# An encoder block on one core: SSD decay moved off GpSimd, skip factors in the vector load, the last units by token tile, VectorE's order at the FFN's entry

## The chip, the core and the metric

The kernel runs on one core of a Trainium2 chip. Its engines each work through a queue of their own, in order: TensorE (PE in the profile) for matrix products, with its weight loads shown as PEld; VectorE (DVE), ScalarE (ACT) and GpSimd (POOL) for elementwise work; SyncE (SP), which here only issues DMAs. The metric is the device time of one execution in microseconds (us).

## What is computed

One layer of a hybrid encoder on 256 tokens of width 2048, in float32. Cut to what matters here:

```python
h = rms_norm(x, norm_mix_pre)
q, k, v, z, xbc, dt, g_sb, g_ssd = split(h @ w_in)
o_sb = stick_breaking_attention(q, k, v)               # 16 heads x 128
xs, bm, cm = split(silu(causal_dwconv(xbc, ...)))      # 64 heads x 64, 8 groups
dt = softplus(dt + dt_bias); a = -exp(a_log)
# SSD: decay = exp(cs_i - cs_j) where j <= i, else 0 (cs: cumulative sum of dt * a)
y = ssd_scan(xs, dt, a, bm, cm)                        # (cm.bm * decay) @ (xs * dt) per head
y = rms_norm_per_group((y + xs * d_skip) * silu(z))
merged = sigmoid(g_sb) * (o_sb @ w_sb_proj) + sigmoid(g_ssd) * (y @ w_ssd_proj)
x = x + rms_norm(merged @ w_out, norm_mix_post)
h = rms_norm(x, norm_ffn_pre)
gate, val = split(causal_dwconv(h @ w_up, ...))        # 2 x 5632
x = x + rms_norm((gelu(gate) * val) @ w_down, norm_ffn_post)
```

## The kernel before

**Weights.** All weights stream once, as 715 units of 128x1024 floats. A unit is loaded by SP (`raw`), rounded by ACT to `whi` (L63) and completed by VectorE with the rest, `wlo` = raw - whi (L64); both halves go to PE, which makes a float32 product of three faster ones. `unit()` (L97) hands a unit to PE's code and has three more prepared ahead; five buffers hold raw units, five hold split ones.

**Products.** `tok_mm` (L136) gives tokens by features: two PSUM banks, one for each token tile t of 128 tokens, three products for each step of 128 inputs and each t (L145 to L147), 12 for a unit. `feat_mm` (L115) gives features by tokens with pairs of products (L112, L113), 8 pairs for a unit; each pair needs both token tiles of its activations. `feat_mms` (L123) runs over the four chunks of its activations in the outer loop, two banks inside.

**Order.** PE's queue is as the program writes it. On the other engines a scheduler of the framework orders the work, save inside `manual_schedule`, where ACT and VectorE keep the written order: at the start (L189), at the FFN's entry (L619) and at the end (L713). Work on the side is written as generators; `pump()` (L155) advances the first of them by one `yield` after each four steps of `tok_mm`, or after a `feat_mm`.

**Stages.** Start: x is loaded in four chunks and multiplied by the norm's gain (`a`); x by tokens (`xt`) comes later for the statistics; ten products on `wake` keep PE busy meanwhile. Then eight SSD groups: `feat_mm` for xs and for B and C (`bc`), `tok_mm` for z, and beside ps_z the generator `ssd_work` (L323). In it PE transposes xs into px; `xw` = px * dt; `xd` (shown as xs) = px * d_skip, a copy on ACT and a product on GpSimd; `mm` is made from csb - cs by a subtraction (L338), masked by GpSimd's affine_select (L339), run through Exp on ACT as one 128x2048 operation (L347) and multiplied by pcb = B.C on VectorE (L350). ACT copies a part of pcb into `xw` (L345), the operand of po (L353). po carries the state of the first token tile to the second, pd (L363) is the part inside a tile. csb is the cumulative sum, spread over partitions by a DMA through DRAM. Then gates, attention, merging, and ps_mo, the product with w_out.

**The FFN's entry** (L618 to L652). After the last ps_mo: squares of its two banks (`n1.add`, n_j), `last` (n_v, then Ln and Exp on ACT), `newton` (three small operations on VectorE) give `n1.r`. Then for each feature block n and token tile t: mog = mog * r + xg (L632), transposed by PE (pth), rounded by ACT and completed by VectorE into the activations `h` (L64). ps_f, the first two tiles of the FFN, follow. x itself (xn, L647) and its statistics come after.

**The tail** (L713 to L727). After the last ps_fo: squares of both banks, `gained` (L701), `last`, `newton`, nine adds (L726), each with a store of its block, from ACT's queue and SP's in turn.

## Time and profile before

| | us |
|---|---|
| median of three runs | 2100.75 (2100.36 to 2102.08) |
| the profiled run's own time | 2101.31 |
| its span | 2099.6 |
| PE busy | 2072.1 (99%) |
| VectorE busy | 1386.0 (66%) |
| ACT busy | 1156.9 (55%) |
| GpSimd busy | 152.3 (7%) |

The span runs from the first instruction to the last; the profiled run's time has 1.7 us around it. Busy PE is not PE at its peak: where the clock is granted at half, products take twice as long and count as busy. In the rows below L12 is line 12 of the kernel, x4 a count of instructions merged into one row, and the brackets tell how long the engine stood before the row and what ended that.

### The profile page before, as it was taken

To read this page: it belongs to the slowest core of one execution; us is meant where nothing else is said; L and a number is where in the kernel's file an instruction comes from. 1 tells how busy PE (TensorE), PEld (TensorE's weight loads), DVE (VectorE), ACT (ScalarE), POOL (GpSimd) and SP (SyncE) were. 2 spreads that over 40 slices of the span, in tenths; PEclk is the share of its full clock that TensorE was granted. 3 is DMA by queue.
4 is the path that set the end of the run, shared out by engine and by line. 5 is a ranking of instruction groups with operands and counts; after the bars stand their busy time and mean duration, and the time that the engine had idled before them with its cause. 6 is when DMAs were issued, how large, how long until landed. Compare 5 with 4: busy or idle time off the path is not lost.

```text
span 2099.6 us, 27950 instructions
## 1 busy us (share of the span) xinstructions
PE 2072.1 (99%) x10632; PEld 1760.7 (84%) x10632; DVE 1386.0 (66%) x1794; ACT 1156.9 (55%) x1542; POOL 152.3 (7%) x134
## 2 busy tenths in 40 slices
PE   9999999999999999999999999999999999999997
PEld 7788888888888888888888888788888888888886
DVE  6888877788544445555544566598878887854443
ACT  6767677667543334555556444475555555544442
POOL 0222102222000000000000021100000000000000
PEclk9999999999999999999999999999999999999999
DMA  8564565555555555555555746475555555565653
GB/s 297 194 205 160 190 205 186 176 199 179 187 197 192 192 194 186 180 171 171 170 172 185 274 161 210 141 250 191 189 190 190 189 189 190 191 232 202 195 193 109
DMA packets 109094, 402.79 MB, mean 192 GB/s; under 512 B 12416, under 2 KB 12672, under 8 KB 106656
## 3 DMA queue, kind: packets, MB, share of 16 engines
q1 hardware_dynamic: 104912, 380.07, 54.1%
q0 software_dynamic: 3328, 20.02, 2.7%
q8 instruction: 83, 1.36, 0.3%
q10 hardware_dynamic: 720, 0.93, 0.1%
q14 instruction: 51, 0.42, 0.1%
HBM read 396.71 MB, written 4.26 MB: 191 GB/s over the span
## 4 chain that ended last, share of the span: by engine, by line
PE 92%; POOL 2%; DVE 2%; issue 2%; DMA 1%; ACT 1%; SPq 0%; DVEq 0%; ACTq 0%; POOLq 0%
PE ps_fv L112 8%; PE ps_fg L112 8%; PE ps_qk L112 6%; PE ps_xs L112 5%; PE ps_fo L147 4%; PE ps_fo L145 4%; PE ps_fo L146 4%; PE ps_fg L113 4%; PE ps_fv L113 4%; PE ps_qk L113 3%; PE ps_ssd L147 3%; PE ps_ssd L145 3%; PE ps_ssd L146 3%; PE ps_xs L113 2%; PE ps_bc L112 2%; PE ps_z L146 2%
## 5 line engine op out<-in xcount | busy, mean ns | idle before, releaser
L64 DVE TENSOR_TENSOR wlo<-raw,whi 128x1024 fp32r<-128x1024 f32 (+1 forms) x715 | 905.1, 1270 | 601.2 <-ACT whi L63 600.6
L63 ACT CAST whi<-raw 128x1024 fp32r<-128x1024 f32 (+1 forms) x715 | 746.2, 1051 | 793.7 <-PE ps_fo L147 128.9
L112 PE MATMUL ps_fg<-h,whi 128*128 128x512 f32 x688 | 240.7, 394 | 0.0
L112 PE MATMUL ps_fv<-h,whi 128*128 128x512 f32 x688 | 240.6, 394 | 0.0
L113 PE MATMUL ps_fg<-h,wlo 128*128 128x256 f32 x688 | 190.6, 277 | 0.0
L113 PE MATMUL ps_fv<-h,wlo 128*128 128x256 f32 x688 | 190.6, 277 | 0.0
L112 PE MATMUL ps_qk<-a,whi 128*128 128x512 f32 x512 | 181.3, 398 | 0.0
L112 PE MATMUL ps_xs<-a,whi 128*128 128x512 f32 x464 | 162.9, 396 | 0.0
L112 PEld LDWEIGHTS ps_fv<-h,whi 128*128 128x128 f32 x688 | 129.0, 188 | 30.0
L112 PEld LDWEIGHTS ps_fg<-h,whi 128*128 128x128 f32 x688 | 129.0, 188 | 30.0
L113 PE MATMUL ps_qk<-a,wlo 128*128 128x256 f32 x512 | 143.5, 280 | 0.0
L145 PE MATMUL ps_fo<-whi,f 128*128 128x512 f32 x352 | 136.9, 389 | 0.0
L147 PE MATMUL ps_fo<-whi,f 128*128 128x512 f32 x352 | 136.9, 389 | 0.0
L146 PE MATMUL ps_fo<-wlo,f 128*128 128x512 f32 x352 | 136.9, 389 | 0.0
L113 PEld LDWEIGHTS ps_fg<-h,wlo 128*128 128x128 f32 x688 | 129.2, 188 | 0.0
L113 PEld LDWEIGHTS ps_fv<-h,wlo 128*128 128x128 f32 x688 | 129.2, 188 | 0.0
L113 PE MATMUL ps_xs<-a,wlo 128*128 128x256 f32 x464 | 129.0, 278 | 0.0
L112 PEld LDWEIGHTS ps_qk<-a,whi 128*128 128x128 f32 x512 | 96.1, 188 | 22.6
L145 PE MATMUL ps_z<-whi,a 128*128 128x512 f32 x256 | 103.7, 407 | 0.0
L112 PEld LDWEIGHTS ps_xs<-a,whi 128*128 128x128 f32 x464 | 87.1, 188 | 19.6
L146 PE MATMUL ps_z<-wlo,a 128*128 128x512 f32 x256 | 100.4, 392 | 1.0 <-DVE wlo L64 1.0
L147 PE MATMUL ps_z<-whi,a 128*128 128x512 f32 x256 | 100.1, 391 | 0.0
(282 smaller groups left out, 3832.5 us busy)
## 6 DMA issues: line engine op xcount, KB each, us to landing
raw<-wts SPq DMA_DIRECT2D x713, 512.0 KB, 3.8
csb<-cs_dram POOLq DMA_DIRECT2D x8, 1024.0 KB, 8.1
xt<-xN SPq DMA_DIRECT2D x2, 1024.0 KB, 10.6
csb<-gain POOLq DMA_DIRECT2D x8, 256.0 KB, 4.1
xn<-xN POOLq DMA_DIRECT2D x2, 1024.0 KB, 7.9
x_dram<-xn POOLq DMA_DIRECT2D x2, 1024.0 KB, 9.0
xe<-x_dram POOLq DMA_DIRECT2D x2, 1024.0 KB, 10.3
x<-xT SPq DMA_DIRECT2D x3, 512.0 KB, 9.2
```

The source lines that it names most:

```text
L63: nc.scalar.copy(hi, src)
L64: nc.vector.tensor_tensor(lo, src, hi.bitcast(F32), op=ALU.subtract)
L112: nc.tensor.matmul(ps, hi[:, w], act[:, k % 4, :, :].rearrange("p s t -> p (s t)"), start=(k == 0), stop=last)
L113: nc.tensor.matmul(ps[:, :T], lo[:, w], act[:, k % 4, 0, :], start=False, stop=last, skip_group_check=True)
L145: nc.tensor.matmul(pss[t], ah, hi[:, w], start=(k == 0), stop=False)
L146: nc.tensor.matmul(pss[t], ah, lo[:, w], start=False, stop=False)
L147: nc.tensor.matmul(pss[t], al, hi[:, w], start=False, stop=(k == nk - 1))
```

## The change

- **Start.** x0 comes in one load, ahead of raw0's halves; 12 products on `wake` instead of 10; the d_skip factors, spread over partitions, are appended to the vector load, and the GpSimd DMA of dsk goes.
- **SSD.** GpSimd's products, masks and addition in `ssd_work` go. VectorE makes px * d_skip straight from PSUM, the decay product and the addition. Instead of masking before Exp, ACT takes Relu(-(csb - cs)) and Exp(-that), for each token tile on its own; the mask (m_le) multiplies pcb (`cbm`), 128x128 for each tile. pcb's products move ahead to the stretch behind px, and pd comes one more `yield` behind po.
- **FFN's entry.** `tok_mm_lag` is used for the last ps_mo: in the last three units it does t=0 first and then the 18 products of t=1. The statistics are made for each tile on its own, and the order on ACT and VectorE is written out anew; two units are prepared at its head (`ready()`).
- **Tail.** `tok_mm_lag` for the last ps_fo, and statistics, adds and stores tile by tile.

```diff
+    def tok_step(pss, acts, k, nk, t, hi, lo):
...
+    def tok_mm_lag(acts, nk, name, lag=3):
+
+        pss = [mm_bank(f"{name}_{t}") for t in range(2)]
+        held = []
+        for k in range(nk):
+            left = (nk - 1 - k) // 2
+            if k % 2 == 0:
+                w = unit(min(WBUFS - 2, left) if left < lag else WBUFS - 2)
+            if left < lag:
+                held.append((k, w))
+                tok_step(pss, acts, k, nk, 0, *w)
+            else:
+                for t in range(2):
+                    tok_step(pss, acts, k, nk, t, *w)
+        for k, w in held:
+            tok_step(pss, acts, k, nk, 1, *w)
         return pss
...
-    for i in range(10):
+    for i in range(12):
...
+    nc.sync.dma_start(x_raw[0], xT[:, 0:4, :])
     for i in range(2):
-        nc.sync.dma_start(x_raw[0][:, 2 * i:2 * i + 2, :], xT[:, 2 * i:2 * i + 2, :])
         nc.sync.dma_start(raw0[:, i * 512:i * 512 + 512], wts[0][:, i * 512:i * 512 + 512])
...
-    dsk = const.tile([P, 64], F32, name="dsk")
-    nc.gpsimd.dma_start(dsk, dskip.partition_broadcast(P))
+    dsk = vec[:, C_D:C_D + 64]
...
-            nc.scalar.copy(xd[:, t, :], px)
-            nc.gpsimd.tensor_tensor(v3(xd[:, t, :]), v3(xd[:, t, :]), bc_in(dsk[:, h8], 64), op=ALU.mult)
-        nc.gpsimd.tensor_tensor(v3(xw[:, 2, :]), v3(xw[:, 0, :]), bc_in(dec0[:, h8], 64), op=ALU.mult)
-        for t in range(2):
-            nc.vector.tensor_tensor(mm[:, t, :, :], csb[:, :, t * P:(t + 1) * P], bc_in(cs_tok[:, t, h8], P), op=ALU.subtract)
-            nc.gpsimd.affine_select(out=mm[:, t, :, :], in_=mm[:, t, :, :], pattern=[[0, 8], [1, P]], compare_op=ALU.is_ge,
-                                    fill=-30000.0, base=0, channel_multiplier=-1)
-        yield
+            nc.vector.tensor_tensor(v3(xd[:, t, :]), v3(px), bc_in(dsk[:, h8], 64), op=ALU.mult)
         pcb = paux.tile([P, 512], F32, tag="aux", name=f"pcb{g}")
...
+        cbm = xw[:, 3, P:3 * P]
         nc.scalar.copy(xw[:, 3, 0:P], pcb[:, P:T])
+        for t in range(2):
+            nc.vector.tensor_tensor(cbm[:, t * P:(t + 1) * P], pcb[:, 256 * t:256 * t + P], m_le, op=ALU.mult)
         lnexp()
-        nc.scalar.activation(mm, mm, AF.Exp)
-        for t in range(2):
-            cb = pcb[:, 256 * t:256 * t + P].unsqueeze(1).broadcast_to([P, 8, P])
+        for t in range(2):
+            m = mm[:, t, :, :]
+            nc.vector.tensor_tensor(m, csb[:, :, t * P:(t + 1) * P], bc_in(cs_tok[:, t, h8], P), op=ALU.subtract)
+            nc.scalar.activation(m, m, AF.Relu, scale=-1.0)
+            nc.scalar.activation(m, m, AF.Exp, scale=-1.0)
+        nc.vector.tensor_tensor(v3(xw[:, 2, :]), v3(xw[:, 0, :]), bc_in(dec0[:, h8], 64), op=ALU.mult)
+        yield
+        for t in range(2):
+            cb = cbm[:, t * P:(t + 1) * P].unsqueeze(1).broadcast_to([P, 8, P])
             nc.vector.tensor_tensor(mm[:, t, :, :], mm[:, t, :, :], cb, op=ALU.mult)
...
-        nc.gpsimd.tensor_tensor(xd[:, 1, :], xd[:, 1, :], off, op=ALU.add)
+        nc.vector.tensor_tensor(xd[:, 1, :], xd[:, 1, :], off, op=ALU.add)
+        yield
         yield
...
-        ps = tok_mm(m_ch, KT, f"ps_mo{n}")
+        ps = (tok_mm if n < 3 else tok_mm_lag)(m_ch, KT, f"ps_mo{n}")
...
+        def scaled(n, t):
+            d = mog[t][:, blk(n)]
+            nc.vector.scalar_tensor_tensor(d, d, n1.r[:, t:t + 1], xg[t][:, blk(n)], op0=ALU.mult, op1=ALU.add)
+            pts[n, t] = transposed(d, paux, "tp", f"pth{n}_{t}")
+
+        def halves(n, t):
+            split_chunk(h_ch[n], t, pts.pop((n, t)))
+
+        def by_gain(t):
+            nc.vector.tensor_tensor(mog[t][:, blk(3)], ps[t], gfp[:, blk(3)], op=ALU.mult)
+
+        def ready():
+            for _ in prep():
+                pass
+
+        def stats(t):
+            n1.add(3, t, ps[t])
+            n1.last(slice(t, t + 1))
+
+        ready()
+        ready()
+        stats(0)
+        n1.newton(slice(0, 1))
+        scaled(0, 0)
+        scaled(1, 0)
+        halves(0, 0)
+        scaled(2, 0)
+        halves(1, 0)
+        stats(1)
+        halves(2, 0)
+        n1.newton(slice(1, 2))
+        scaled(0, 1)
+        by_gain(0)
+        halves(0, 1)
+        scaled(1, 1)
+        ready()
+        halves(1, 1)
+        scaled(3, 0)
+        scaled(2, 1)
+        halves(3, 0)
+        by_gain(1)
+        halves(2, 1)
+        ready()
+        scaled(3, 1)
+        halves(3, 1)
...
-        n3.add(3, 0, ps[0])
-        n3.add(3, 1, ps[1])
-        gained(3, 0, gfo)
-        n3.last()
-        gained(3, 1, gfo)
-        n3.newton()
-        for n in range(4):
-            for t in range(2):
+        for t in range(2):
+            w = slice(t, t + 1)
+            n3.add(3, t, ps[t])
+            gained(3, t, gfo)
+            n3.last(w)
+            n3.newton(w)
+            for n in range(4):
```

At the FFN's entry, the rows of PE from the last products of ps_mo (t=1) to the first of ps_f; before:

```order
L145 MATMUL ps_mo_1_10904<-whi_10979,m_10396 128x512
L146 MATMUL ps_mo_1_10904<-wlo_10980,m_10396 128x512
L147 MATMUL ps_mo_1_10904<-whi_10979,m_10396 128x512
L385 MATMUL pth_0_11068<-ident,mog_10412 128x128 x4
L385 MATMUL pth_1_11074<-ident,mog_10413 128x128 x4
L385 MATMUL pth_0_11080<-ident,mog_10412 128x128 x4
L385 MATMUL pth_1_11086<-ident,mog_10413 128x128 x4
L385 MATMUL pth_0_11094<-ident,mog_10412 128x128 x4
L112 MATMUL ps_f_0_11186<-h_11049,whi_10997 128x512
```

and now (pth_0 is of t=0, pth_1 of t=1):

```order
L140 MATMUL ps_mo_1_10879<-whi_10954,m_10371 128x512
L141 MATMUL ps_mo_1_10879<-wlo_10955,m_10371 128x512
L142 MATMUL ps_mo_1_10879<-whi_10954,m_10371 128x512
L410 MATMUL pth_0_11033<-ident,mog_10387 128x128 x4
L410 MATMUL pth_0_11039<-ident,mog_10387 128x128 x4
L410 MATMUL pth_0_11047<-ident,mog_10387 128x128 x4
L410 MATMUL pth_1_11065<-ident,mog_10388 128x128 x4
L113 MATMUL ps_f_0_11167<-h_11006,whi_11014 128x512
```

All products of t=1's bank still stand ahead of the first transpose; four transposes, three of t=0 and one of t=1, stand ahead of ps_f where there were five.

ACT at the same place, from the squares (n_j) of the two banks on; before:

```order
L571 ACTIVATE n_j_11055,n_ss<-ps_mo_0_10903 128x512
L571 ACTIVATE n_j_11057,n_ss<-ps_mo_1_10904 128x512
L590 ACTIVATE n_q<-n_v 128x2
L591 ACTIVATE n_r<-n_q 128x2
L63 CAST h_11049<-pth_0_11068 128x4x128
L63 CAST h_11049<-pth_1_11074 128x4x128
L63 CAST h_11050<-pth_0_11080 128x4x128
```

and now:

```order
L596 ACTIVATE n_j_11024,n_ss<-ps_mo_0_10878 128x512
L616 ACTIVATE n_q<-n_v 128x1
L617 ACTIVATE n_r<-n_q 128x1
L64 CAST h_11006<-pth_0_11033 128x4x128
L64 CAST h_11007<-pth_0_11039 128x4x128
L596 ACTIVATE n_j_11054,n_ss<-ps_mo_1_10879 128x512
L616 ACTIVATE n_q<-n_v 128x1
L617 ACTIVATE n_r<-n_q 128x1
L64 CAST h_11008<-pth_0_11047 128x4x128
L64 CAST h_11006<-pth_1_11065 128x4x128
```

The square of the second bank now stands behind the roundings of two blocks of t=0, and the third such rounding behind the second tile's Exp.

VectorE there, now, from the second tile's n_v to its first scaled block (L651, which was L632) and on:

```order
L615 SCALAR_TENSOR_TENSOR n_v<-n_ss,n_v 128x1
L65 TENSOR_TENSOR h_11008<-pth_0_11047,h_11008 128x4x128
L621 TENSOR_TENSOR n_q<-n_r 128x1
L622 SCALAR_TENSOR_TENSOR n_q<-n_q,n_v 128x1
L623 SCALAR_TENSOR_TENSOR n_r<-n_q,n_r 128x1
L651 SCALAR_TENSOR_TENSOR mog_10388<-mog_10388,n_r,xg_10381 128x512
L658 TENSOR_TENSOR mog_10387<-ps_mo_0_10878,gfp 128x512
L65 TENSOR_TENSOR h_11006<-pth_1_11065,h_11006 128x4x128
```

An `h` of t=0 (L65, which was L64) stands between the second tile's n_v and its newton (L621 to L623).

In the SSD, VectorE in group 4 from the first px on; before:

```order
L333 TENSOR_TENSOR xw_2996<-px_0_2998,dt_tok 128x512
L333 TENSOR_TENSOR xw_2996<-px_1_3006,dt_tok 128x512
L338 TENSOR_TENSOR mm_2997<-csb_2955,cs_tok 128x1024 x2
L64 TENSOR_TENSOR wlo_3044<-raw_3041,whi_3043 128x1024
L64 TENSOR_TENSOR wlo_3070<-raw_3067,whi_3069 128x1024
L350 TENSOR_TENSOR mm_2997<-mm_2997,pcb_3059 128x1024 x2
```

and now:

```order
L355 TENSOR_TENSOR xw_2983<-px_0_2985,dt_tok 128x512
L356 TENSOR_TENSOR xs_2944<-px_0_2985,vec 128x512
L355 TENSOR_TENSOR xw_2983<-px_1_2992,dt_tok 128x512
L356 TENSOR_TENSOR xs_2944<-px_1_2992,vec 128x512
L363 TENSOR_TENSOR xw_2983<-pcb_2999,m_le 128x128 x2
L367 TENSOR_TENSOR mm_2984<-csb_2942,cs_tok 128x1024 x2
L370 TENSOR_TENSOR xw_2983<-xw_2983,dec_222 128x512
L65 TENSOR_TENSOR wlo_3034<-raw_3031,whi_3033 128x1024
L374 TENSOR_TENSOR mm_2984<-mm_2984,xw_2983 128x1024
L65 TENSOR_TENSOR wlo_3054<-raw_3051,whi_3053 128x1024
L374 TENSOR_TENSOR mm_2984<-mm_2984,xw_2983 128x1024
```

Two products with the factors of the skip, the masks, the decay product have come between px and the next `wlo`; the products with pcb (L374) are each followed by a `wlo`.

PE in the same group, around pcb, now:

```order
L354 MATMUL px_1_2992<-ident,xf_3_2759 128x128
L140 MATMUL ps_z_0_2945<-whi_2911,a_137 128x512
L141 MATMUL ps_z_0_2945<-wlo_2912,a_137 128x512
L142 MATMUL ps_z_0_2945<-whi_2911,a_137 128x512
L358 MATMUL pcb_2999<-bc_1_2931,bc_0_2860 128x256
L359 MATMUL pcb_2999<-bc_1_2931,bc_0_2860 128x128
L140 MATMUL ps_z_1_2946<-whi_2911,a_137 128x512
```

pcb stood 24 products of ps_z behind px, and stands three behind it.

## Rows read from the trace of the kernel before

**Rows 1.** Page, busy us, share of the span and instructions of the engines.
```profile
PE 2072.1 (99%) x10632; PEld 1760.7 (84%) x10632; DVE 1386.0 (66%) x1794; ACT 1156.9 (55%) x1542; POOL 152.3 (7%) x134
```

**Rows 2.** PE's waits: who waited for whom, us in total, times, longest.
```profile
PE po L353 <- ACT xw L345: 3.7, 6, 0.7
PE pth L385 <- DVE mog L632: 2.9, 1, 2.9
PE ps_first L112 <- DVE a L197: 2.9, 2, 2.1
PE po L353 <- POOL xw L336: 2.4, 1, 2.4
PE ps_z L146 <- DVE wlo L64: 1.0, 1, 1.0
```

**Rows 3.** Timeline of PE, its last products: start, us, what.
```profile
2086.26 0.39 PE L146 MATMUL ps_fo<-wlo,f 128*128 128x512 f32 x1
2086.49 0.39 PE L147 MATMUL ps_fo<-whi,f 128*128 128x512 f32 x1
```

**Rows 4.** Slices: width, busy share (instructions) by engine, PEclk, DMA share, GB/s.
```profile
15.00:16.00 1.00, 1.00 (x6) 0.89 (x5) 1.00 (x2) 0.75 (x2) 0.00 (x0) 0.74 1.02 399
```

**Rows 5.** Timeline of VectorE, start: start, us, what [idle before <- releaser].
```profile
31.94 0.17 DVE L240 TENSOR_SCALAR rx_v<-ss_x 128x2 f32<-128x2 f32 x1 [3.96 <-ACT xt L398]
...
57.46 1.22 DVE L64 TENSOR_TENSOR wlo<-raw,whi 128x1024 fp32r<-128x1024 f32 x1
```

**Rows 6.** DMA, 0 to 22 us: GB/s in 40 slices; packets, MB, share.
```profile
GB/s 0 0 0 45 247 193 280 274 171 93 123 220 339 395 387 413 380 447 402 432 410 425 410 432 402 425 402 404 407 421 382 406 406 398 425 395 432 380 477 372
...
q0 software_dynamic: 32, 0.03, 4.1%
```

**Rows 7.** Timeline of VectorE in SSD group 4.
```profile
315.41 1.28 DVE L333 TENSOR_TENSOR xw<-px,dt_tok 128x512 f32<-128x512 f32 x2
...
320.22 4.09 DVE L64 TENSOR_TENSOR wlo<-raw,whi 128x1024 fp32r<-128x1024 f32 x2
```

**Rows 8.** Timeline of PE in SSD group 4, px.
```profile
314.28 1.04 PE L332 MATMUL px<-ident,xf 128*128 128x128 f32 x8
```

**Rows 9.** Timeline of ACT in SSD group 4.
```profile
315.59 0.42 ACT L318 ACTIVATE bc<-cva 128x256 f32<-128x256 f32 x1
...
325.29 1.91 ACT L347 ACTIVATE mm<-mm 128x2048 f32<-128x2048 f32 x1 [4.84 <-POOL mm L339]
```

**Rows 10.** Timeline of VectorE in SSD group 0.
```profile
80.32 2.36 DVE L338 TENSOR_TENSOR mm<-csb,cs_tok 128x1024 f32<-128x1024 f32 x2 [3.63 <-DMA csb<-cs_dram]
...
87.64 2.35 DVE L350 TENSOR_TENSOR mm<-mm,pcb 128x1024 f32<-128x1024 f32 x2 [2.33 <-ACT mm L347]
```

**Rows 11.** Timeline of PE at the FFN's entry.
```profile
1349.70 0.39 PE L147 MATMUL ps_mo<-whi,m 128*128 128x512 f32 x1
...
1356.97 0.48 PE L112 MATMUL ps_f<-h,whi 128*128 128x512 f32 x1
...
1369.66 0.40 PE L112 MATMUL ps_fg<-h,whi 128*128 128x512 f32 x1
```

**Rows 12.** Slices at the FFN's entry, columns as in rows 4.
```profile
1353.00:1354.00 1.00, 0.96 (x6) 0.75 (x7) 1.00 (x2) 0.34 (x1) 0.00 (x0) 0.77 0.00 0
1356.00:1357.00 1.00, 1.00 (x8) 0.84 (x6) 1.00 (x3) 0.73 (x2) 0.00 (x0) 0.52 0.00 0
```

**Rows 13.** Timeline of VectorE at the FFN's entry.
```profile
1350.84 0.16 DVE L589 SCALAR_TENSOR_TENSOR n_v<-n_ss,n_v 128x2 f32<-128x2 f32 x1
...
1352.10 2.74 DVE L632 SCALAR_TENSOR_TENSOR mog<-mog,n_r,xg 128x512 f32<-128x512 f32 x4
...
1366.88 4.05 DVE L647 SCALAR_TENSOR_TENSOR xn<-mo,n_r,xn 128x512 f32<-128x512 f32 x6
```

**Rows 14.** Timeline of ACT at the FFN's entry, the first rounding of a block.
```profile
1353.66 0.59 ACT L63 CAST h<-pth 128x512 fp32r<-128x512 f32 x1 [2.19 <-PE pth L385]
```

**Rows 15.** Timeline of VectorE in the tail, the nine adds.
```profile
2088.89 5.52 DVE L726 SCALAR_TENSOR_TENSOR fo<-fo,n_r,xe 128x512 f32<-128x512 f32 x9
```

More of the change, by code (lines that the diff above doesn't have):

```diff
@@ L38, in block_kernel @@
 @with_exitstack
-def block_kernel(ctx, tc, xT, xN, wts, vecs, rows, hvec, dskip, gain, out):
+def block_kernel(ctx, tc, xT, xN, wts, vecs, rows, hvec, gain, out):
     nc = tc.nc
@@ L134, in feat_sum @@
         nc.vector.tensor_tensor(dst, dst, ps[:, :T], op=ALU.add)
+    def tok_step(pss, acts, k, nk, t, hi, lo):
+        w = slice(k % 2 * 512, k % 2 * 512 + 512)
+        ah, al = (acts[k // 4][:, k % 4, s, t * P:(t + 1) * P] for s in range(2))
+        nc.tensor.matmul(pss[t], ah, hi[:, w], start=(k == 0), stop=False)
+        nc.tensor.matmul(pss[t], ah, lo[:, w], start=False, stop=False)
+        nc.tensor.matmul(pss[t], al, hi[:, w], start=False, stop=(k == nk - 1))
     def tok_mm(acts, nk, name):
@@ L619, in block_kernel @@
     with tc.manual_schedule(engines=ACT_DVE):
-        n1.add(3, 0, ps[0])
-        n1.add(3, 1, ps[1])
-        nc.vector.tensor_tensor(mog[0][:, blk(3)], ps[0], gfp[:, blk(3)], op=ALU.mult)
-        n1.last()
-        nc.vector.tensor_tensor(mog[1][:, blk(3)], ps[1], gfp[:, blk(3)], op=ALU.mult)
-        n1.newton()
-        pts = {}
-        lag = 3
-        for i in range(8 + lag):
-            if i < 8:
-                n, t = divmod(i, 2)
-                d = mog[t][:, blk(n)]
-                nc.vector.scalar_tensor_tensor(d, d, n1.r[:, t:t + 1], xg[t][:, blk(n)], op0=ALU.mult, op1=ALU.add)
-                pts[i] = transposed(d, paux, "tp", f"pth{n}_{t}")
-            if i >= lag:
-                n, t = divmod(i - lag, 2)
-                split_chunk(h_ch[n], t, pts.pop(i - lag))
+        pts = {}
+        def scaled(n, t):
[38 more added lines that the diff above has]
+        halves(3, 1)
         for t in range(2):
@@ L705, in block_kernel @@
         nc.gpsimd.dma_start(gfo, rows[2, blk(n)].partition_broadcast(P))
-        ps = tok_mm(f_ch, FF_T, f"ps_fo{n}")
+        ps = (tok_mm if n < 3 else tok_mm_lag)(f_ch, FF_T, f"ps_fo{n}")
         if n < 3:
```

32 lines of the change are left out of this document (16 added, 16 removed).

## The prediction

> **What bounds the kernel now.** I read the page's busy shares first: TensorE (PE) is busy for 2072.1 of 2099.6 us [rows 1], so the only time that can be won is the 27.5 us in which it stands, plus what it runs at half clock. The view of PE's waits [rows 2] says where it stands. Reader, see two things: there are only a few entries, and each sits at one place that the change touches. At the start PE waits 2.9 us for `a`. At the first ps_z it waits 1.0 for a `wlo`. In SSD group 0 it waits 2.4 for GpSimd's `xw`, in six later groups 3.7 together for ACT's copy into `xw`. At the FFN's entry it waits 2.9 for `mog`. What is left, some 13 us, lies behind the last matmul, in the tail. Where PE runs, one product follows the other every 0.227 us [rows 3]. I take these places in order of time. The profiled run took 2101.31 us (span 2099.6), 0.56 above the median of 2100.75; changes are worked out on the profiled run and carried to the median.
>
> **Start.** Before, x0 and raw0 come in alternating halves, and PE waits 2.1 of its 2.9 us for the second half of `a`; after that wait the clock is at half until well into the slice 15 to 16 us, mean 0.74 there [rows 2, 4]. The change sends x0 whole and ahead, keeps PE on `wake` for two more products, and drops the 32 KB dsk load (its queue: 4.1% of the DMA engines' time over 22 us, so 0.9 us of each) [rows 6]. For PE alone this could be worth 2.1 us of wait and about 2.7 of half clock. I don't count that, because PE is not late here: VectorE is. The loads run back to back at some 400 GB/s [rows 6], xt last; VectorE waits 3.96 us for the statistics of xt and then works nearly without a gap until the `wlo` of 57.46, for which PE waits 1.0 till 58.7 [rows 2, 5]. A PE that arrives earlier waits longer there. What remains is by how much the stream of loads moves: at least half of the 0.9 us of dsk, at most that and the dip of four slices in which 171, 93, 123 and 220 GB/s flowed and not some 400 (0.55 us each, so 1.4 us lost) [rows 6]. I take **-1.5 us**, ends -0.4 and -2.2; to +0.2 if the longer wait at 58.7 lowers the clock, as the 2.9 us wait at the FFN's entry did (rows below).
>
> **SSD group 0.** Here the chain is the decay: csb lands, VectorE's two subtractions start at 80.32 after 3.63 us of waiting for that DMA, GpSimd masks (4 us), ACT's Exp, VectorE's product at 87.64 [rows 10], pd. Now ACT does the mask as a Relu in two halves of about 1 us each, each behind its own subtraction, and the product of the first half need not wait for the second. From 80.32: two subtractions 2.36, Relu and Exp of the second half some 2.0, one product 1.2 with a `wlo` (1.22) between: pd can begin at about 87.0 where it could not before the first product's end, near 88.9; PE would get there at 86.7. The 2.4 us wait for GpSimd's xw goes as well, though what it gave away was partly time in which PE would have waited for pd. I take **-2.0**, ends -0.5 (a `wlo` or a table load in ACT's queue comes between) and -2.4 (the row).
>
> **SSD groups 1 to 7.** The six waits of po sum to 3.7 us [rows 2]: ACT's copy L345 comes only after the Exp, which waits 4.84 us for GpSimd's mask [rows 9]. In the new order that copy comes before Relu and Exp, so this goes: -3.7. The price: pcb's products no longer follow 24 products after the px transposes but three, as the order shows, some 1.6 us after px starts (0.8 for the transposes, 3 x 0.227) [rows 8]. They need the silu of bc, which ended 1.73 us after px started, at 316.01 [rows 9]; ACT's queue ahead of it is as before. So a new wait of 0.1 to 0.4; I take 0.3, in seven groups +2.1. VectorE takes over four things per group: two skip products (0.64 each, by the pair of 1.28 in [rows 7]), the decay product and the addition (0.6 to 0.7 each), two masks of 128x128 (0.3 each). Against these 3.2 us stand its own gains: with GpSimd at work a pair of `wlo` takes 4.09 [rows 7], one alone 1.22 [rows 5], so 1.7 per pair, and about 1.3 on the subtractions likewise. VectorE's load is about unchanged, but now some 6 us (2.6 + 0.6 + 2.36 + 0.64) come in one block with no `wlo` in it. With the next `wlo` that is 7.4, inside the lead of three units (12 products of 0.227 each, 8.2 us), so PE doesn't see it. Sum **-1.6**, ends -3.7 (silu comes in time) and +2.
>
> [...]
>
> **FFN's entry.** This term decides. Call T1 the end of the last ps_mo product, 1349.70 + 0.39 = 1350.09 [rows 11]. Before, PE stands 2.9 us [rows 2], transposes at half clock and starts ps_f at T1+6.9; the first ps_fg is at T1+19.6. The change holds back the last 18 products of t=1 (18 x 0.227 = 4.1 us), so that t=0's statistics and its first two `scaled` are done by T1. But the order shows where the transposes are: PE runs in order, and all 18 products stand ahead of pth of t=0. Nothing of t=0 is transposed under them. And ACT now has two CASTs of t=0 ahead of t=1's Square. Step by step from T1, with 0.5 us for four transposes ([rows 8], 8 in 1.04), 0.6 for a CAST [rows 14], 0.6 to 0.68 for a VectorE operation of 128x512 and 1.26 from n_v to the first `scaled` [rows 13]: pth(0,0), pth(1,0) T1 to 0.9; their CASTs to 1.6; Square of t=1 1.6 to 2.3; VectorE does halves(0,0), scaled(2,0), halves(1,0) until 3.1 and only then n_v; Exp ends at 3.7; CAST of (2,0), queued behind Exp, to 4.3; halves(2,0) to 4.9, and newton of t=1 stands behind it, to 5.5; scaled(0,1), pth(0,1) 6.4 to 6.9, CAST 7.6, halves 8.4. The first ps_f needs this: **T1+8.4**, where it was T1+6.9. The t=0 work that was to be early is early; but the first ps_f wants both tokens, and t=1's chain became longer. From there the 32 pairs and the late chunks take 13.7 us (before 12.7; h of (1,1) and (3,1) come late), first ps_fg T1+22.1 at full clock. That is +2.5.
>
> Two further prices. First, only one unit of ps_fg is split ahead of the six L647 operations (4.05 us [rows 13]); before, two were. The second unit's `wlo` then ends 1.9 us after PE has used up the first (8 x 0.353): +1.9. Second, the clock. Before, one wait of 2.9 us was enough for half clock: the mean is 0.77 in the slice from 1353 and still 0.52 in that from 1356 [rows 12]. Now PE has three gaps, 1.9, 3.1 and 1.6, with half a microsecond of transposes between them. I let it fall as early as before (T1+3.4) and stay at half until 2 to 3 us after ps_f has begun: that delays the late transposes and the first pairs by 1.7. Sum **+6.1**; ends +2.5 (full clock, and the second unit covered) and +7.6 (half clock until T1+14.5).
>
> [...]
>
> **Tail.** Before, the scaled adds start at 2088.89, 2.0 us after the last ps_fo (2086.49 + 0.39 [rows 3]), and nine take 5.52, to 2094.41 [rows 15]; the span ends 5.2 after that, 12.7 after the last product. After, t=0's four adds run under and just behind t=1's held products, so 1 MB is on its way early. For t=1: ACT's second store waits for the third add of t=0, and Square of t=1 stands behind it, at +1.0; `gained` after it to +2.4, n_v to newton +3.6, three adds and two halves 2.9: +6.5 instead of +7.5. The queues then hold half as much; I let the end come 4.6 after the last add instead of 5.2. **-1.6**, ends -1.0 (only the adds) and -2.6.
>
> **Sum.** -1.5 - 2.0 - 1.6 + 6.1 - 1.6 = -0.6: the profiled run 2100.7, the median 2100.75 - 0.6 = **2100.2 us**.
>
> **Rivals.**
> - *A, cheap entry.* The clock stays up and the second unit is covered: the entry costs +2.5, the time is 2096.6. For it: PE does some work in each gap. Against: [rows 12], one such gap was enough.
> - *A2, the change does what it says at the entry*: transposes of t=0 hide, the 2.9 wait and the 1.7 of half clock go: -4.6 instead of +6.1, 2089.5. Against: the order of PE, and Square of t=1 behind two CASTs. My forecast is thus that the entry does not do what the words say.
> - *C, the start keeps all it wins.* If VectorE is not what PE meets at 58.7, 4.8 instead of 1.5 is won: 2096.9. Against: VectorE's nearly gapless stretch from 31.94 on.
> - *B, slower: VectorE starves PE in the SSD groups.* If the subtractions stay as slow as they were beside GpSimd (an estimate from the `wlo` pair, 1.7 us more per pair) and pcb comes 0.5 late, the block is 8.2 and with its `wlo` 9.4 us, 1.2 over the lead: seven groups wait 8.4 us, in place of -1.6, and the time is 2110.2. It decides from a block of 7 us. For it: VectorE takes 3.2 us more per group. Against: a pair alone takes 2.36 [rows 10], and nothing is left on GpSimd beside it.
>
> **Chances.** Forecast (2097 to 2104 by its terms' ends) 0.69, A 0.12, A2 0.06, C 0.06, B 0.07. A measurement tells 0.2% (4.2 us) from no change. Faster: A2, half of A and of C, and a little of the forecast's low edge: 0.19. Slower: B and the forecast's high edge: 0.10. Same 0.71. The range leaves out A2 and B and the outer part of A: 2095.5 to 2105.
>
> **What would show it.** After the change: first ps_f 8 to 9 us behind the last ps_mo and the first ps_fg at 22 to 25 (right), or below 7 (A2); PE waiting about 2 us for the second unit's `wlo` of ps_fg; half clock in the slices behind T1+3.5; no wait of po, and 0.3 us waits of pcb for `bc`; a wait of more than 2 us at the first ps_z; the last add 6.5 us behind the last ps_fo. I am wrong if ps_f starts early, or if waits for `wlo` show in the SSD groups.

## The result: slower by 0.25%, outside the range

| | before | after |
|---|---|---|
| median of 20 runs each, us | 2101.44 (2099.53 to 2106.69) | 2108.93 (2100.43 to 2113.08) |
| ratio of after to before, by the means | | 1.0025 [1.0014, 1.0037] |
| the profiled run's own time, its span | 2101.31, 2099.6 | 2111.94, 2110.2 |

The forecast was 2100.2 us, within 2095.5 to 2105. The 20 times of after fall into two groups: nine lie at 2100.4 to 2102.9 us, eleven at 2108.8 to 2113.1, and the profiled run is one of the eleven.

**The page of after**, busy us, share and instructions of each engine, against [rows 1]:

```profile
PE 2084.6 (99%) x10636; PEld 1766.3 (84%) x10636; DVE 1380.0 (65%) x1850; ACT 1155.7 (55%) x1547; POOL 63.1 (3%) x85
```

GpSimd lost 89 us, VectorE 6 although it took over GpSimd's work. PE, however, is busy 12.5 us longer, with four more instructions (the two more products on `wake`, two instructions each). The span grew by 10.6, and the time in which PE stands fell from 27.5 to 25.6. So the time did not come as waits; it is in products that ran longer or further apart.

**PE's waits in after** (who waited for whom, us in total, times, longest), against [rows 2]:

```profile
PE pth L410 <- DVE mog L651: 4.7, 2, 3.0
PE pcb L358 <- ACT bc L339: 2.0, 6, 0.3
PE ps_fg L114 <- DVE wlo L65: 1.8, 1, 1.8
PE ps_f L113 <- DVE h L65: 1.6, 2, 1.4
PE ps_z L141 <- DVE wlo L65: 1.2, 1, 1.2
...
PE pd L388 <- DVE mm L374: 0.6, 1, 0.6
```

Most waits moved as the prediction had it: po's are gone, pcb's of 0.3 have come, pth waits twice, the second unit of ps_fg waits 1.8. One sign did not come: the first ps_z waits 1.2, where more than 2 was named. One wait was not foreseen: group 0's pd, which runs at the start of group 1, waits 0.6 for `mm`. No `wlo` of an SSD group behind that first ps_z is in the list.

**Where the 10.6 us came in.** The first product of four stages, timeline of PE (start, us, what). Before:

```profile
51.64 0.39 PE L145 MATMUL ps_z<-whi,a 128*128 128x512 f32 x1
...
82.51 0.39 PE L112 MATMUL ps_xs<-a,whi 128*128 128x512 f32 x1
...
788.22 0.39 PE L112 MATMUL ps_qk<-a,whi 128*128 128x512 f32 x1
...
1847.33 0.39 PE L145 MATMUL ps_fo<-whi,f 128*128 128x512 f32 x1
```

and after, the same four and the last ps_fo:

```profile
48.84 0.39 PE L140 MATMUL ps_z<-whi,a 128*128 128x512 f32 x1
...
77.33 0.39 PE L113 MATMUL ps_xs<-a,whi 128*128 128x512 f32 x1
...
782.65 0.39 PE L113 MATMUL ps_qk<-a,whi 128*128 128x512 f32 x1
...
1860.03 0.40 PE L140 MATMUL ps_fo<-whi,f 128*128 128x512 f32 x1
...
2099.23 0.39 PE L142 MATMUL ps_fo<-whi,f 128*128 128x512 f32 x1
```

Read the differences down: -2.80 at the end of the start, -5.18 where group 1 of the SSD begins, -5.57 behind the SSD, and then +12.70 at the end of the FFN's pairs. The last product ends at 2099.62, the span 10.58 behind it, where it was 12.7: -2.1. So the start, the SSD and the tail gave what was forecast or a little more, and 18.3 us were lost between 1344 and 1860 us. The entry itself is the next thing to read, PE in after:

```profile
1344.15 0.39 PE L142 MATMUL ps_mo<-whi,m 128*128 128x512 f32 x1
...
1347.13 0.63 PE L410 MATMUL pth<-ident,mog 128*128 128x128 f32 x4 [1.71 <-DVE mog L651]
1350.71 1.09 PE L410 MATMUL pth<-ident,mog 128*128 128x128 f32 x4 [2.95 <-DVE mog L651]
1353.19 0.80 PE L113 MATMUL ps_f<-h,whi 128*128 128x512 f32 x1 [1.40 <-DVE h L65]
...
1369.45 0.40 PE L113 MATMUL ps_fg<-h,whi 128*128 128x512 f32 x1
...
1375.11 0.38 PE L114 MATMUL ps_fg<-h,wlo 128*128 128x256 f32 x1 [1.83 <-DVE wlo L65]
```

T1 is now 1344.15 + 0.39 = 1344.54. The first ps_f stands at T1+8.65 (T1+6.88 before), the first ps_fg at T1+24.9 (T1+19.57). The slices of after give the clock (the last three columns: PEclk, DMA share, GB/s):

```profile
1350.00:1352.00 2.00, 1.09 (x4) 0.72 (x4) 1.16 (x2) 0.17 (x1) 0.00 (x0) 0.50 0.00 0
1358.00:1360.00 2.00, 2.00 (x13) 1.79 (x12) 0.37 (x1) 0.00 (x0) 0.00 (x0) 0.76 0.03 10
1376.00:1378.00 2.00, 2.00 (x9) 1.71 (x8) 2.00 (x5) 1.16 (x3) 0.00 (x0) 0.51 0.87 274
```

0.50 is half clock. The clock is there from T1+4.2 to T1+14.4, and again from 1376.0 to 1379.5, just behind the wait for the second unit. The pairs of ps_f take 0.64 us at it (from 1356.13 to 1358.69) and 0.353 at 1.00 (from 1360.40 to 1363.93), so 1.8 times as long; ahead of the prediction I wrote twice. At 1384.61 (T1+40.1) the last product of the first ps_fg and ps_fv starts, where before it was T1+30.8: the entry costs **+9.3**. The other **+9.0** of the 18.3 come later, in 475 us without a wait. Where nothing waits, the two kernels run the same code, yet not at the same rate. The slice from 1500 to 1600 us, before:

```profile
1500.00:1600.00 100.00, 100.00 (x579) 87.45 (x578) 80.53 (x127) 57.22 (x90) 0.00 (x0) 1.00 0.58 190
```

and after:

```profile
1500.00:1600.00 100.00, 100.00 (x569) 86.77 (x568) 79.33 (x126) 55.57 (x87) 0.00 (x0) 1.00 0.56 185
```

PE is busy all the time in both, at full clock in both, and 579 products fall into the slice before, 569 after. That is 1.8% in the pairs of the FFN.

### The profile page after: what moved, and what is told of

Its sections match the earlier page's. It is cut to its first block, busy times and chain, and to the rows that moved or that the text cites. A ratio compares the mean times of both kernels' runs of the same rounds, so it can differ in the third digit from the quotient of the medians.

```text
span 2110.2 us, 27913 instructions
## 1 busy us (share of the span) xinstructions
PE 2084.6 (99%) x10636; PEld 1766.3 (84%) x10636; DVE 1380.0 (65%) x1850; ACT 1155.7 (55%) x1547; POOL 63.1 (3%) x85
## 4 chain that ended last, share of the span: by engine, by line
PE 93%; DVE 3%; DMA 2%; issue 1%; ACT 1%; SPq 0%; DVEq 0%; ACTq 0%
PE ps_fv L113 8%; PE ps_fg L113 8%; PE ps_qk L113 6%; PE ps_xs L113 5%; PE ps_fv L114 4%; PE ps_fg L114 4%; PE ps_fo L140 4%; PE ps_fo L141 4%; PE ps_fo L142 4%; PE ps_qk L114 3%; PE ps_ssd L141 3%; PE ps_ssd L142 3%; PE ps_ssd L140 3%; PE ps_bc L113 2%; PE ps_xs L114 2%; PE ps_z L141 2%
## 5 line engine op out<-in xcount | busy, mean ns | idle before, releaser
L65 DVE TENSOR_TENSOR wlo<-raw,whi 128x1024 fp32r<-128x1024 f32 (+1 forms) x715 | 885.2, 1241 | 633.1 <-ACT whi L64 632.6
L64 ACT CAST whi<-raw 128x1024 fp32r<-128x1024 f32 (+1 forms) x715 | 747.3, 1050 | 824.7 <-PE ps_fo L142 128.9
L113 PE MATMUL ps_fg<-h,whi 128*128 128x512 f32 x688 | 246.4, 400 | 0.0
L113 PE MATMUL ps_fv<-h,whi 128*128 128x512 f32 x688 | 245.1, 399 | 0.0
```

Of the source, the lines that this page charges most:

```text
L64: nc.scalar.copy(hi, src)
L65: nc.vector.tensor_tensor(lo, src, hi.bitcast(F32), op=ALU.subtract)
L113: nc.tensor.matmul(ps, hi[:, w], act[:, k % 4, :, :].rearrange("p s t -> p (s t)"), start=(k == 0), stop=last)
```

## The experiments

**Theory R (rhythm).** The pairs of `feat_mm` (one product of 512 columns with `whi`, one of 256 with `wlo`) run in one of two rhythms. In before, behind 1381.22, the `whi` products start at 1383.14, 1383.49, 1383.83, 1384.18: 0.35, 0.34, 0.35 apart, a mean of (1847.33 - 1381.22)/1344 = 346.8 ns a pair up to the first ps_fo.

In after they are 0.36, 0.35, 0.35 apart, a mean of (1860.03 - 1386.57)/1340 = 353.3 ns. Timeline of PE in after, `whi` products alone:

```profile
1388.33 0.40 PE L113 MATMUL ps_fg<-h,whi 128*128 128x512 f32 x1
...
1388.69 0.40 PE L113 MATMUL ps_fg<-h,whi 128*128 128x512 f32 x1
...
1389.04 0.40 PE L113 MATMUL ps_fg<-h,whi 128*128 128x512 f32 x1
```

6.6 ns in 1340 pairs are 8.8 us. I call them the fast and the slow rhythm. The trace of before holds both: its pairs ahead of r_ps take 353.2 ns, those behind it 346.7, and in attention 127 pairs of ps_qk from 788.22 on take 353.2 and 31 from 874.5 on 346.6; after has the same two at the same places (from 782.65 and 868.89 on). In these traces a rhythm mostly lasts until something that is no pair breaks in (run 5 has an exception). In the FFN the last thing that does is r_ps (L253 before, L274 after; its operand is r_dg), two small products that carry the second norm's factor. Where r_ps stands is set by the framework's scheduler, which shifts single products on PE. Ahead of the prediction I wrote that PE's queue is as the program writes it, and that is wrong in such places. Before, r_ps stands between two units, thus between two pairs:

```profile
1380.86 0.28 PE L113 MATMUL ps_fv<-h,wlo 128*128 128x256 f32 x1
1380.97 0.60 PE L253 MATMUL r_ps<-r_dg,ones 128*128 128x256 f32 x2
1381.22 0.58 PE L112 MATMUL ps_fg<-h,whi 128*128 128x512 f32 x1
```

After, it stands inside the fourth pair of the second ps_fg, between its `whi` and its `wlo` product:

```profile
1385.79 0.39 PE L113 MATMUL ps_fg<-h,whi 128*128 128x512 f32 x1
1386.03 0.59 PE L274 MATMUL r_ps<-r_dg,ones 128*128 128x256 f32 x2
1386.27 0.47 PE L114 MATMUL ps_fg<-h,wlo 128*128 128x256 f32 x1
1386.57 0.39 PE L113 MATMUL ps_fg<-h,whi 128*128 128x512 f32 x1
```

Theory R: r_ps between two pairs sets the fast rhythm; inside a pair it leaves the rhythm as it was. **Rival E (entry):** the loss belongs to the new order at the entry, through its waits, its clock, or units that arrive late afterwards, and r_ps is a bystander. Of PE's products only r_ps is moved in the first two runs below.

**1. After, with r_ps between two pairs.**

```diff
-        nc.tensor.matmul(ps, hi[:, w], ...)
+        m = nc.tensor.matmul(ps, hi[:, w], ...)
+        if state.pop("pin", False):       # first product behind r_ps
+            tc.keep_in_program_order(m)
```

> The kernel after, with one thing fixed: the product r_ps (r2 spread over partitions) stands between two pairs of ps_fg again, as in the kernel before, and not between the whi and the wlo product of one pair. Theory 'rhythm': pairs of the FFN run either in a cycle of two pairs (346.7 ns a pair) or of three (353.3 ns), and what breaks in last settles which; so all runs are near 2102 (2100.5 to 2103.5) and the profile shows 346.7 ns a pair in ps_fg and ps_fv, 1344 pairs x 6.6 ns = 9 us less than the profiled run after (span about 2101). Rival 'entry': the longer entry itself (its falls of the clock, the wait for the second unit) leaves the slow rhythm, wherever r_ps stands; then about half of the runs stay at 2109 to 2112.

Measured: median of 12 runs 2103.67 us, ratio 1.0019 [1.0006, 1.0033]; nine at 2102.2 to 2105.2, three at 2112.8 to 2116.0. The profiled run's span is 2101.8, its pairs take 346.7 ns. r_ps now comes earlier than its operand and PE waits for it:

```profile
1385.26 0.67 PE L276 MATMUL r_ps<-r_dg,ones 128*128 128x256 f32 x2 [0.67 <-DVE r_dg L275]
```

Nine of twelve runs are short, against nine of twenty in after; by itself that proves little. In the profiled run the pairs ahead of r_ps are fast already (0.34 to 0.35 apart from 1382.69 on). The three long runs, of which there is no trace, suggest that the place between pairs is not enough when PE waits in front of it.

**2. Before, with r_ps inside a pair.** PE's other products keep their order, and the entry is the old one; behind r_ps a few operations on ACT and VectorE change places.

```diff
+        if "r" in state and k == 3:
+            r = state.pop("r")            # order only: whi, r_ps, wlo
+            for x, y in ((r, a), (b, r)):
+                tc.add_manual_dep(x.ins, y.ins.name, ...)
```

> The kernel before with r_ps held until it stands between the whi and the wlo product of the fourth pair of the next ps_fg, as in the kernel after; nothing else on TensorE moves. Theory 'rhythm': the slow cycle of 353.3 ns appears in the FFN in some or all runs, which then take 9 us more (2109 to 2111). Rival 'entry': stays at 2100 to 2103, 346.7 ns.

Measured: 2109.68 us (2109.36 to 2111.22, 5 runs), ratio 1.004 [1.0027, 1.0053]. PE around r_ps:

```profile
1381.39 0.39 PE L112 MATMUL ps_fg<-h,whi 128*128 128x512 f32 x1
1381.62 0.59 PE L257 MATMUL r_ps<-r_dg,ones 128*128 128x256 f32 x2
1381.86 0.47 PE L113 MATMUL ps_fg<-h,wlo 128*128 128x256 f32 x1
```

The slice from 1500 to 1600 us of this run, columns as above:

```profile
1500.00:1600.00 100.00, 100.00 (x567) 86.69 (x567) 78.70 (x124) 56.68 (x90) 0.00 (x0) 1.00 0.57 187
```

The kernel before, with its old entry, becomes as slow as after. Before had 2101.2 in the same comparison; rival E can't explain these 8.5 us, theory R does. That the few moved operations are not the cause is shown by run 6.

**3. After, with the old entry** (`tok_mm` for the last ps_mo, and before's order on ACT and VectorE).

```diff
-        ps = (tok_mm if n < 3 else tok_mm_lag)(m_ch, KT, f"ps_mo{n}")
+        ps = tok_mm(m_ch, KT, f"ps_mo{n}")
```

> The kernel after with the FFN's entry of the kernel before (tok_mm for the last ps_mo, statistics of both tiles together, the old order on ACT and VectorE); start, SSD and tail as after. My sum by the two traces: start and SSD -5.6, tail -2.1, so 7.7 below before: 2093.5 (2092 to 2095), T1 to the first ps_fg 19.6 us as before, and r_ps between two pairs, fast rhythm. Rival 'given back': what start and SSD win is lost again at the FFN's entry because VectorE or a load is the bound there; then 2098 to 2101.

Measured: 2095.53 us, 9 of 12 runs at 2093.4 to 2096.8, the others 2102.2 to 2107.3; ratio 0.9982 [0.9968, 0.9996]. Here r_ps stands between two pairs too, behind a wait of 0.4 us. Against run 1, which has the new entry and mostly the fast rhythm, that is 8.1 us. So both theories hold a part: the rhythm has some 9 us, and the new entry, by itself, 8.

**4. The second unit first** (run 1, and one more unit prepared ahead of the six L704 operations, L647 before).

```diff
-        while state["u"] <= state["at"] + 4:
+        while state["u"] <= state["at"] + 5:
```

> Like e1, and a second unit of the first ps_fg is split ahead of the six operations on xn (L704). Theory: the wait of 1.8 us for that wlo goes, and with it the second fall of the clock (3.4 us at half, 1.7 lost): 3.5 less than e1, about 2098.7. Rival: the six operations, their statistics and r_ps come 1.2 us later and PE waits there instead: within 1 us of e1.

A miss, of the rival too: 2115.02 us (2106.8 to 2117.64, 6 runs), ratio 1.0054 [1.0037, 1.0071]. The longest of PE's waits between 1340 and 1400:

```profile
PE r_ps L276 <- DVE r_dg L275: 5.0, 1, 5.0
```

The second unit's wait is gone, as meant (ps_fg waits 0.2 us in all). But the unit pushed x's statistics back on VectorE, and r_ps, pinned where it was, waited 5.0 us for them. Half clock came with it (0.50 in the slice 1388 to 1390), and the rhythm behind it was the slow one (567 products from 1500 to 1600).

**5. After, and run 3, with r_ps late**: between the 8th and the 9th pair of the second ps_fg, where its operand is ready.

```diff
+        if k == 8 and "r" in state:       # 9th pair stays behind r_ps
+            behind(a, state.pop("r"))
...
+        if k == 7 and "r" in state:       # r_ps stays behind the 8th pair
+            behind(state["r"], b)
```

After:

> The kernel after with r_ps between the eighth and ninth pair of the second ps_fg. Theory: no wait, fast rhythm in all runs, 2101.5 to 2103.5, the price of the entry alone (8 us above e5). Rival chance: part of the runs near 2110 to 2113, as in e1 (3 of 12).

Measured: 2102.44 us (2101.53 to 2104.42, 11 runs), ratio 1.0004 [0.9995, 1.0013]. All eleven runs lie together, where after had eleven long ones of twenty; the profile has 579 products from 1500 to 1600. In it the pairs ahead of r_ps are fast already (0.34 to 0.35 apart), so this profile does not show r_ps ending a slow rhythm; the times do, as far as after's share of long runs is no chance.

With the old entry:

> e2 (start, SSD and tail of the change, the FFN's entry of before), with r_ps held until it stands between the eighth and ninth pair of the second ps_fg, where its operand has long been ready. In e2 r_ps waited 0.4 us for its operand, and 3 of 12 runs were 8 to 13 us slower than the rest. Theory: a break that waits starts the next stretch at a moment that varies, and so in either rhythm; one that does not wait and stands between two pairs gives the fast one. Then all runs are at 2093 to 2096, 346.7 ns a pair. Rival: which rhythm comes is chance of the run, whatever breaks in; then again a quarter of the runs is near 2103 to 2107.

Measured: 2095.0 us (2092.84 to 2096.03, 5 runs), ratio 0.9968 [0.9955, 0.998]: shorter than both kernels. Here the pairs turn from slow to fast eight pairs ahead of r_ps, at the first pair of the second ps_fg (1376.59) and with no wait in the list; from 1500 to 1600 there are 579 products. So r_ps is not the only thing that can change a rhythm. The two kernels differ by the entry alone: 2102.44 - 2095.0 = **7.4 us**. Between 1340 and 1400 PE's waits with the old entry are one line, where after has three lines with 8.1 us (4.7, 1.8 and 1.6):

```profile
PE pth L418 <- DVE mog L667: 3.5, 2, 2.9
```

**6. Before, with r_ps between the 4th and 5th pair.** This asks whether it is the distance or the place in the pair.

```diff
+        if k == 4 and "r" in state:
+            behind(a, state.pop("r"))
...
+        if k == 3 and "r" in state:
+            behind(state["r"], b)
```

> The kernel before with r_ps held four pairs longer, as in e3, but set between the fourth and fifth pair instead of inside the fourth. Theory: what counts is the place within the pair, not the delay; fast rhythm, 2099.5 to 2103, no run near 2110. Rival: the delay counts; 2109 to 2111 as e3.

Measured: 2101.47 us (ten of 11 runs at 2100.33 to 2102.64, one at 2106.06), ratio 1.0 [0.9991, 1.0009]. Ahead of r_ps the pairs are slow, behind it fast (span 2099.7, where before has 2099.6 and run 2 2108.0):

```profile
1382.12 0.40 PE L115 MATMUL ps_fg<-h,whi 128*128 128x512 f32 x1
1382.36 0.28 PE L118 MATMUL ps_fg<-h,wlo 128*128 128x256 f32 x1
1382.47 0.59 PE L260 MATMUL r_ps<-r_dg,ones 128*128 128x256 f32 x2
1382.71 0.59 PE L115 MATMUL ps_fg<-h,whi 128*128 128x512 f32 x1
```

Half a pair away from run 2, and 8.2 us below it. In the two traces the order of the operations is the same on PE, VectorE, ACT and GpSimd, r_ps alone excepted. This pair of runs leaves neither the entry nor the other engines' order as a cause.

**7. After, r_ps inside the seventh pair.** If a place inside a pair always made the slow rhythm, all runs should be long; by theory R it depends on what ran ahead of it.

```diff
+        if "r" in state and k == 6:
+            r = state.pop("r")
+            for x, y in ((r, a), (b, r)):
+                tc.add_manual_dep(x.ins, y.ins.name, ...)
```

> The kernel after with r_ps three pairs later, between the whi and the wlo product of the seventh pair of the second ps_fg. In the kernel after, 11 of 20 runs had the slow rhythm and 9 the fast one; r_ps stands there 0.9 us behind its operand. Theory 'a wait decides': where r_ps is inside a pair and never waits, all runs are slow, as in e3: 2109 to 2113. Rival 'the place inside a pair leaves it to chance' in this kernel: again some runs near 2101 to 2103.

Measured: 2102.43 us, 9 of 11 runs at 2100.3 to 2104.3, two at 2110.1 and 2112.0; ratio 1.001 [0.9998, 1.0023]. In the profiled run the starts are 0.35 and 0.34 apart ahead of r_ps already, and stay so:

```profile
1384.13 0.39 PE L113 MATMUL ps_fg<-h,whi 128*128 128x512 f32 x1
...
1384.47 0.39 PE L113 MATMUL ps_fg<-h,whi 128*128 128x512 f32 x1
1384.70 0.59 PE L278 MATMUL r_ps<-r_dg,ones 128*128 128x256 f32 x2
1384.95 0.47 PE L114 MATMUL ps_fg<-h,wlo 128*128 128x256 f32 x1
```

So r_ps inside a pair doesn't make the slow rhythm; it fails to end it. Before's pairs ahead of r_ps run slow (run 2 stays slow in all five). After's, which come behind a wait for a unit and mostly a change of the clock, come in either rhythm (slow in after's profile, fast in those of the runs 1, 5 and 7), and r_ps inside the pair leaves them so. Why two of eleven runs are long here and eleven of twenty in after is not shown.

**8. Another entry.** Here the Square of t=1 comes ahead of the roundings of t=0 on ACT (r_ps as in 5).

```diff
         scaled(0, 0)
         scaled(1, 0)
-        halves(0, 0)
         scaled(2, 0)
-        halves(1, 0)
         stats(1)
-        halves(2, 0)
+        by_gain(1)
         n1.newton(slice(1, 2))
         scaled(0, 1)
-        by_gain(0)
+        halves(0, 0)
...
         halves(0, 1)
```

> e6 with another order at the FFN's entry: the held products stay, but the statistics of t=1 (square, n_v, Ln, Exp, newton) come on ACT and VectorE ahead of every rounding and completion of t=0, three scaled blocks of t=0 are made under the held products, and scaled(0,1) comes first after newton. By the durations of the traces the first ps_f starts at T1+5.0 (8.65 in the profiled run after, 6.9 before) and the first ps_fg at T1+17.7 to 19 (24.9, 19.6): 1 to 2 us below e5, 2091 to 2093.5. Rival: holding back t=1 is itself the fault, whatever the order: the first ps_f stays later than T1+6.9 and the time above 2096.

Measured: 2097.03 us (2094.7 to 2098.79, 9 runs), ratio 0.9976 [0.9967, 0.9986]; in time a miss, since 2091 to 2093.5 was expected. PE:

```profile
1349.59 0.79 PE L116 MATMUL ps_f<-h,whi 128*128 128x512 f32 x1
...
1369.05 0.57 PE L119 MATMUL ps_fg<-h,wlo 128*128 128x256 f32 x1 [2.15 <-DVE wlo L65]
```

The first ps_f is 3.6 us earlier than in after (1353.19), some 5 us behind the last ps_mo instead of 8.65. Of after's 4.7 us at the transposes 2.2 remain. This confirms that ACT's queue (two roundings ahead of the Square) was what held t=1's statistics. Still, the entry is 3.4 us behind the old one, from the first ps_qk to the first ps_fo: the second unit waits 2.15 us, and half clock follows it (pairs 0.64 us apart from 1369.42 to 1371.99, 0.35 behind).

**9. The same, with a unit prepared between the six L704 operations.** Two more things differ: r_ps stands between the 8th and 9th pair of the second ps_fv, and PE's pairs there are held in the written order.

```diff
         for n in range(4):                # x's blocks
...
+            if n == 0:
+                ready()
```

> e7, and the second unit of the first ps_fg is split after two of the six operations on xn, not after all six; r_ps stands between the eighth and ninth pair of the second ps_fv, late enough not to wait. Theory: e7's wait of 2.1 us for that unit's wlo goes, and with it the second fall of the clock (3.4 us at half, 1.7 lost): 2097.0 - 3.8 = 2093.2 (2092 to 2095), the fastest of all, 1 to 2 us below e5. Rival: the wait only moves to the next unit or to r_ps, as it did in e4: 2096 to 2098.

A miss: 2096.39 us (2094.2 to 2099.86, 7 runs), ratio 0.9975 [0.9964, 0.9985], where 2093.2 was expected. The profiled run is the longest of the seven; its ps_qk starts 4.5 us later than in run 8's profile (787.27 against 782.76), with a wait of 1.8 us for group 0's `mm` and half clock from 85.8 to 92.6. The wait was split, not removed, and the clock fell at 1372.6 all the same (0.65 in the slice 1372 to 1374):

```profile
1370.56 0.50 PE L116 MATMUL ps_fg<-h,whi 128*128 128x512 f32 x1 [0.73 <-ACT whi L64]
1371.82 0.39 PE L122 MATMUL ps_fg<-h,wlo 128*128 128x256 f32 x1 [0.76 <-DVE wlo L65]
```

When ps_f starts early, its units are used up early, and ACT and VectorE, which split units and make `h` from the same queues, are late with the next: the order there shifts the lack and doesn't mend it.

**10. Each of the other three parts alone**, on before, r_ps as in 5.

> The kernel before with the change's start alone (x0 whole and first, 12 products on wake, the skip factors in the vector load); r_ps between the eighth and ninth pair of the second ps_fg. Prediction's term: -1.5 (-0.4 to -2.2). By the first ps_z of the profiled run after: -2.8. So 2098.5 to 2100 against e8 and before at 2101.2. Rival: group 0's chain through the statistics of xt takes it back: within 0.5 of before.

> The kernel before with the change's ssd_work alone; r_ps as in e10. Prediction's terms: group 0 -2.0, groups 1 to 7 -1.6, together -3.6: 2097.6. By the profiled run after: group 0 -2.4, groups 1 to 7 -0.4: 2098.4. Rival: VectorE's longer block starves TensorE without the earlier start: 2101 or more, waits for wlo in the groups.

> The kernel before with the change's tail alone (last ps_fo by token tile, statistics, adds and stores tile by tile); r_ps as in e10. Prediction's term -1.6 (-1.0 to -2.6); by the profiled run after 12.7 - 10.6 = -2.1: 2099.1. Rival: the end of the stores is set by the stream of 2 MB, whenever it starts: within 0.5 of before.

| part alone | median us (runs) | ratio | in the profiled run |
|---|---|---|---|
| start | 2100.94 (12, 2097.64 to 2108.03) | 1.0 [0.999, 1.001] | ps_z -2.7, ps_qk -2.8 |
| SSD | 2097.44 (9, 2096.39 to 2098.47) | 0.9977 [0.9967, 0.9986] | group 0 -2.5, ps_qk -3.6 |
| tail | 2099.18 (11, 2096.07 to 2100.42) | 0.9982 [0.9974, 0.9991] | end -2.2 behind the last product |

The SSD alone shows PE's new wait with the old sum gone:

```profile
PE pcb L345 <- ACT bc L326: 2.0, 6, 0.3
```

The start alone keeps its 2.8 us up to ps_qk in the profiled run, but its twelve times scatter over 10 us, and their mean doesn't show a gain; why is open.

## Why the prediction was wrong, point by point

| term | forecast | measured |
|---|---|---|
| start | -1.5 (-0.4 to -2.2) | -2.8 |
| SSD group 0 | -2.0 (-0.5 to -2.4) | -2.4 |
| SSD groups 1 to 7 | -1.6 (-3.7 to +2) | -0.4; alone -1.1 |
| FFN's entry | +6.1 (+2.5 to +7.6) | +9.3 |
| tail | -1.6 (-1.0 to -2.6) | -2.1 |
| r_ps inside a pair | none | +9.0 in the profiled run |
| sum | -0.6 | +10.6 |

**The step that failed is one that is not in the sum: the move of r_ps.** The prediction's first step says that the only time that can be won is the 27.5 us in which PE stands, plus what it runs at half clock. By that it took 1340 pairs, some 470 us busy at full clock, to be equal in both kernels, without a reason given; r_ps is not named. The trace of after shows r_ps inside a pair and these pairs 9.0 us longer. The two rates could be seen ahead: the prediction itself counts 0.353 us a pair at the entry (8 x 0.353), where before's pairs behind r_ps take 0.347. Runs 2, 5 and 6 show what that place is worth: 8.2 us on before (2109.68 with r_ps inside a pair, 2101.47 with it between two), and in after the difference of its own two groups, 8.7 us (medians 2111.11 and 2102.38). Without it, after is at 2102.44 (run 5), 2.2 us above the forecast and inside its range. That is partly luck: by the table the start, group 0 and the tail gave 2.2 us more than forecast, the entry and the other groups took 4.4 more. None of the rivals had this mechanism; that *B* would have given 2110.2 is a coincidence: its mark, waits for `wlo` in the SSD groups, is absent.

**The entry** was right in direction, place and marks, and mis-sized by 3.2 us, beyond its own upper end of +7.6. First ps_f: forecast T1+8.4, found T1+8.65. First ps_fg: within the 22 to 25 named, at its end (24.9). Second unit: 1.9 forecast, 1.83 found. Two terms were short. Half clock lasted until T1+14.4, which is the upper end of the term: +5.3 at the first ps_fg where 2.5 + 1.7 was summed. The 13.7 us from ps_f to ps_fg at full clock can be tested: in the five profiles of the new entry (after and the runs 1, 4, 5 and 7) that stretch took 15.5 to 16.3 us with 4.1 to 5.8 us of half clock in it, 0.46 us more for each us of that, and the line through them comes to 13.6 at none (an estimate from these profiles). So in after half clock took some 2.6 where 1.7 was summed. That it would end 2 to 3 us after ps_f's begin was my estimate, which no row gave; it took 5.8. And the wait for the second unit had a price of its own that I did not add: behind it the clock fell again, 1376.0 to 1379.5, for 1.7 us. Of the 9.3, 0.5 is not assigned.

My reason for the second unit's wait was also worded wrongly: in both kernels one unit is split ahead of the six operations; what differs is that VectorE is later against PE: the six begin 2.8 us ahead of the first ps_fg before, 0.4 behind it after.

Runs 3 and 5 size the entry from outside, by medians: 7.4 to 8.1 us. That is between the forecast and the profiled run's 9.3, which is on the high side: to the same place the profiles of the runs 5 and 7 take 0.8 and 1.6 us less. In run 7's the second unit's wait, 1.78 us, left the clock at full.

Nor was one gap always enough for half clock, as the prediction had it against *A*: with before's entry the wait of 2.9 us left the clock at 1.00 in the profiles of run 6 and of run 5's old entry. There ps_f starts at T1+6.7 and takes the same 12.7 us to ps_fg, so before's half clock was worth 0.2 us, not the 1.7 that *A2* gave back. *A* (cheap entry) and *A2* (transposes hidden) are out: pth waits 4.7 us, not 2.9.

**The chain at the entry** was read rightly off the order. ACT's timeline shows the two roundings ahead of the Square of t=1, and VectorE's newton (1349.24) began only when the `h` of 1348.63 was done:

```profile
1345.01 1.07 ACT L64 CAST h<-pth 128x512 fp32r<-128x512 f32 x2 [3.17 <-PE pth L410]
1345.97 0.61 ACT L596 ACTIVATE n_j<-ps_mo 128x512 f32<-128x512 f32 x1
```

**The start** kept more than forecast: ps_z comes 2.8 us earlier and waits 1.2 for its `wlo` against 1.0, so VectorE came earlier too; a part of rival *C*. **Group 0** was right up to the first product of group 1. **Groups 1 to 7**: both marks came as worked out (po's 3.7 gone, pcb's 2.0 against the 2.1 forecast, though the 1.6 us worked out for pcb's place, 0.8 and three products of 0.227, are 1.5), and the net is 0.5 to 1.2 us short. Of the 1.2 in after, 0.5 is group 0's pd, which waits 0.64 where it waited 0.11; that wait differs from profile to profile (0 to 1.8) and is none in that of the SSD alone. In after the first fifteen pairs of ps_xs of a group run in the slow rhythm (from 266.41 on 350, 361 and 349 ns apart in turn), in before fast (from 273.20 on 350 and 343); that is some 0.1 us a group at 6.6 ns each and would be most of the rest. It was read from the traces, and no run isolates it. **The tail** was right by its own steps: the last add ends 6.46 us behind the last ps_fo (6.5 forecast),

```profile
2103.21 2.87 DVE L782 SCALAR_TENSOR_TENSOR fo<-fo,n_r,xe 128x512 f32<-128x512 f32 x5
```

and the span ends 4.1 behind it, where 4.6 was taken and 5.2 was before.

**What stays open.** Why the phase of one small product selects the rhythm, and why after's pairs ahead of r_ps come in either (nine runs short, eleven long): I only argue that the breaks ahead of it, which wait and change the clock, fall differently from run to run. Two of the eleven times of run 7, and the longest of the start alone, have no trace to read.
